# Last down products and second norm of a decoder layer: four equal column chunks, centred weights, row sums made in DRAM

## Chip, cores and metric

The kernel runs on one core of a Trainium2 chip. The metric is device time in microseconds, the median over the runs shown; the profile is of one more execution.

## The reference

One layer of a hybrid decoder, for a prompt of 1,024 tokens and 8 sample tokens that share the weights. Three branches (a gated recurrence, windowed attention, attention into 256 memory tokens) are merged, and then two post-norm steps follow. The change concerns the last of them:

```
h = layer_norm(ALPHA * x + merged @ w_out, ln1_g, ln1_b)
gt, up = jnp.split(h @ w_gate_up, 2, axis=-1)
h = layer_norm(ALPHA * h + (jax.nn.silu(gt) * up) @ w_down, ln2_g, ln2_b)
```

`layer_norm` takes mean and variance over the 1,024 features of each token. The inner width of the gated product is 2,816. All data are 32-bit floats.

## The kernel before, in words

Activations are held transposed: features on the 128 partitions (8 blocks m = 0 to 7 of the model width, 22 blocks of the inner width), tokens along the columns, T = 1,032 of them (1,024 and 8). A layer norm over features is thus a sum over partitions and blocks; it is done by a matrix product with a 128x128 matrix `ones` filled with 1/1024, which leaves the column's mean on every partition.

A product in full precision is done as three fast products: each operand is split into a high part (ScalarE casts, L79) and the rest (VectorE subtracts, L80), and `mm3` (L120 to L122) multiplies high by high, high by low and low by high.

`gate_up_down` (L1236) runs the gate and up products and most of the down product in *units* of a Strassen kind. A unit has seven steps i = 0 to 6 in two column halves, each of 12 products of 128x258 (L245 to L247), so 168 products. The units of the down product are (part, j), part 0 and 1, j = 0 to 3; each covers 8 of the 22 inner blocks and makes output rows 2j and 2j+1 in two tiles, za and zb. Steps put scaled partial results aside (p1s, p5s, u2s, ScalarE, L271) or add them into za and zb (VectorE, L273, L275 and L278; the last half of zb ScalarE, L1461). The PSUM bank that step 0 opened is used again by steps 2, 4 and 6; step 6 may overwrite it only when zb has been made from it by L275. In the profile `uf_6` and the like are the split weights of a step, d with some letters and digits is a split operand, `ubf`, `ucf`, `udf` are PSUM banks. `scr_h`, in DRAM, holds the residual; when za and zb are complete, GpSimd issues a DMA that accumulates each into its row of `scr_h` (`FinishDown.done`, L1465). Operands of the next part are loaded from `scr_f` (rows of the inner activation) and `scr_t` (sums of rows).

The last six inner blocks, 16 to 21, are done as plain products, in `last_products` (L1336). During the last ten steps of the units their inputs are prepared by hand-set steps (L1285 to L1291): six rows of `scr_f` are loaded and split (`last_rows`, L1310; tiles g5, g6, g7, named by the *home*, that is the buffers of finished operands that they take over), weight blocks are loaded by SP and split (`last_weights`, L1319; wl0 to wl7 raw, one per output block, in a ring of six raw buffers), and rows of `scr_h` are loaded as `acc` (`last_acc`, L1331). Then, for each of three column chunks (384, 390, 258) and each output block m, 18 products go to a PSUM bank `dl`, and VectorE adds it to acc (L1366). VectorE sums the rows of acc as it goes. The norm of a chunk (`layer_norm`, L951) runs beside the products of the next chunk: mean by `ones`, subtraction, squares, variance, root, reciprocal, scaling (L973), shift on ScalarE (L1354) and store (L1355).

The last chunk has `last_layer_norm` (L986), since no products follow to hide its norm. It takes an approximate mean away early, by `shift` products (L1013, L1014, L1023) from the first two rows; accumulates sums and sums of squares of what is left (VectorE L1004, GpSimd L1006); gets mean and mean square by `le` products (L1030 to L1033), the variance as a difference (L1037), then root (L1038), subtraction of the mean (L1040), reciprocal (L1041), scaling (L1044), shift and store.

What orders the work around the change: the hand-set steps above, `issue_after`, which puts norm pieces behind a named product on each engine, the ring of six raw weight buffers, ten buffers of 1,032 columns for za, zb and acc, and PSUM banks (`mm` 3, `s` 2, `t` 2, `o` 1). Each engine works its own instruction queue in order; SP and GpSimd issue DMAs in theirs.

Of the kernel before, what the change touches and what calls it, by code (L numbers as in the profile page):

```python
# [18 lines left out]
P = 128  # L19
# [7 lines left out]
WIDE = 400  # L27
# [8 lines left out]
LATE = 4  # L36
# [25 lines left out]
class Builder:  # L62
# [87 lines left out]
    def setup(self):  # L150
# [9 lines left out]
        self.shift = self.cst.tile([P, P], F32R, name="shift")  # L160
        nc.vector.memset(self.shift.bitcast(F32), -1.0 / (256 * SHARE))
# [789 lines left out]
    def layer_norm(self, c, r, s1, gcol, emit, name, late=False):  # L951


        nc, ph = self.nc, self.ph
        n = r[0].shape[1]
        yield
        mu = self.col_mean(s1, n, f"{name}mu{c}")
        s2 = ph.tile([P, WIDE], F32, tag="s2", name=f"{name}s2{c}", bufs=1)[:, :n]
        for m in range(KT):
            nc.vector.tensor_sub(r[m], r[m], mu)  # L960
            sq = s2 if m == 0 else ph.tile([P, WIDE], F32, tag="sq", name=f"{name}sq{c}_{m}", bufs=2)[:, :n]
            nc.scalar.activation(sq, r[m], AF.Square)
            if m:
                nc.vector.tensor_add(s2, s2, sq)
        yield
        var = self.col_mean(s2, n, f"{name}va{c}")
        rs = ph.tile([P, WIDE], F32, tag="rs", name=f"{name}rs{c}", bufs=1)[:, :n]
        nc.scalar.activation(rs, var, AF.Sqrt, bias=self.vec[:, V_EPS:V_EPS + 1])
        if late:
            yield  # L970
        nc.vector.reciprocal(rs, rs)
        for m in range(KT):
            nc.vector.scalar_tensor_tensor(r[m], r[m], self.vec[:, gcol + m:gcol + m + 1], rs, op0=ALU.mult,  # L973
                                           op1=ALU.mult)
            emit(m, r[m])

# [8 lines left out]

    def last_layer_norm(self, n, r, product, gcol, emit):  # L986


        nc, ph = self.nc, self.ph
        ones = self.ones.bitcast(F32)  # L990
        tile_ = lambda tag, name, bufs, dt=F32: ph.tile([P, WIDE], dt, tag=tag, name=name, bufs=bufs)[:, :n]
        s1, s2 = tile_("s1", "ls1", 1), tile_("s2", "ls2", 1)
        hi, lo = (t.rearrange("p k n -> p (k n)")[:, :n] for t in self.slot_pairs(4, "c0")[0])
        e1, e2 = self.bank("t", "le1")[:, :n], self.bank("t", "le2")[:, :n]

        def account(m):
            sq = s2 if m == 0 else tile_("sq", f"lsq{m}", 2)
            nc.scalar.activation(sq, r[m], AF.Square)
            if m == 7:
                return sq  # L1000
            if m == 1:
                nc.vector.tensor_add(s1, r[0], r[1])
            elif m:
                nc.vector.tensor_add(s1, s1, r[m])  # L1004
            if m:
                nc.gpsimd.tensor_add(s2, s2, sq)  # L1006

        for m in range(KT):
            ps = product(m, last=m < LATE)
            if m in NORM_AT:  # L1010
                self.norm_step()
            if m >= LATE:
                nc.tensor.matmul(ps, self.shift, hi, start=False, stop=False)  # L1013
                nc.tensor.matmul(ps, self.shift, lo, start=False, stop=True)  # L1014
            nc.vector.scalar_tensor_tensor(r[m], ps, SHARE, r[m], op0=ALU.mult, op1=ALU.add)
            if m == 1:
                s = tile_("xres", "lc0", 2)
                nc.vector.tensor_add(s, r[0], r[1])
                self.split(hi, lo, s)
            elif m == LATE - 1:  # L1020
                with self.tc.issue_after(self.last_mm):
# [591 lines left out]
```

## Time and profile before

| | us |
|---|---|
| median of 3 runs | 1939.35 (1938.84 to 1944.86) |
| profiled execution | 1941.62 |
| its span | 1939.8 |
| first of the last products | 1848.11 |
| last of the last products ends | 1919.43 |
| last store's affine ends | 1936.55 |

The span is what the profile covers, the profiled execution's own time is 1.8 us longer. Rows of a timeline give the start, the busy time, the engine, the line of the kernel, and output from inputs; in square brackets stands how long the engine was idle before and what ended that. Durations of TensorE's products overlap, so starts are to be compared rather than durations; VectorE's and ScalarE's overlap a little too.

### The profile page before, as it was taken

The page shows a single profiled execution, that of the slowest core. Times are in us where ns is not written, and L with a number is a line of the kernel's source. Part 1 is how long each engine was busy: PE and PEld are TensorE (multiplying, and loading weights), DVE is VectorE, ACT ScalarE, POOL GpSimd, SP SyncE. Part 2 cuts the span into 40 slices and gives each one's busy share as a digit, 9 for nine tenths or more (in the row PEclk, how much of TensorE's full clock was granted, in tenths as well). Part 3 has the DMA queues.
Part 4 walks back from the last instruction along what each step waited for, and adds up shares of the span by engine and source line. Part 5 has one row for each costly group of instructions (what it writes and reads, how often), then busy time and mean ns, then how long its engine had stood idle before and what let it go on. Part 6 is the DMA issues. An engine that isn't in the chain of part 4 may idle for free.

```text
span 1939.8 us, 37994 instructions
## 1 busy us (share of the span) xinstructions
PE 1902.9 (98%) x14716; PEld 1872.2 (97%) x14716; DVE 1388.3 (72%) x2738; ACT 1001.3 (52%) x2115; POOL 117.1 (6%) x168
## 2 busy tenths in 40 slices
PE   9999999999999999999999999999999999999996
PEld 9999999999999998988899999999999999999996
DVE  7878987887866655378887557785667667858467
ACT  6555565555655544388775224543433434636424
POOL 1000001110000000022210000000000000001001
PEclk9999999999999999999999999999999999999998
DMA  8545555445523376667534352123245245768542
GB/s 318 175 146 168 169 177 180 137 145 204 183 78 127 126 238 212 201 170 209 152 100 148 110 192 71 50 99 98 88 159 191 100 133 181 256 162 231 137 143 88
DMA packets 171637, 303.20 MB, mean 156 GB/s; under 512 B 19568, under 2 KB 86208, under 8 KB 171456
## 3 DMA queue, kind: packets, MB, share of 16 engines
q1 hardware_dynamic: 168384, 290.22, 45.6%
q0 software_dynamic: 3072, 10.55, 2.8%
q8 instruction: 115, 1.88, 0.4%
q14 instruction: 66, 0.54, 0.1%
HBM read 214.79 MB, written 90.09 MB: 157 GB/s over the span
## 4 chain that ended last, share of the span: by engine, by line
PE 86%; ACT 5%; DVE 4%; DMA 3%; issue 1%; ACTq 0%; SPq 0%; DVEq 0%; POOL 0%; POOLq 0%
PE ub L247 5%; PE ub L245 5%; PE ub L246 5%; PE ubfg L245 4%; PE ubfg L246 4%; PE ubfg L247 4%; PE ud L247 3%; PE ud L246 3%; PE ud L245 3%; PE udfg L245 2%; PE udfg L246 2%; PE udfg L247 2%; PE op L122 2%; PE op L120 2%; PE op L121 2%; PE brs L120 2%
## 5 line engine op out<-in xcount | busy, mean ns | idle before, releaser
L122 PE MATMUL op<-mh,wol 128*128 128x258 f32 x256 | 72.3, 282 | 1.3 <-DVE wol L80 1.3
L120 PE MATMUL op<-mh,woh 128*128 128x258 f32 x256 | 72.5, 283 | 0.0
L121 PE MATMUL op<-ml,woh 128*128 128x258 f32 x256 | 72.1, 282 | 0.0
L602 ACT ACTIVATE bp<-bp,bst 128x257 f32<-128x257 f32 (+1 forms) x128 | 62.8, 493 | 17.6 <-DVE bst L598 17.3
L245 PE MATMUL ub<-th,u_4h 128*128 128x258 f32 x240 | 67.8, 283 | 1.3 <-ACT u2s L271 1.3
L245 PE MATMUL ub<-th,u_0h 128*128 128x258 f32 x240 | 68.0, 283 | 0.6 <-ACT zb L1482 0.5
L247 PE MATMUL ub<-th,u_0l 128*128 128x258 f32 x240 | 68.2, 284 | 0.0
L247 PE MATMUL ub<-th,u_4l 128*128 128x258 f32 x240 | 68.2, 284 | 0.0
L247 PE MATMUL ub<-th,u_2l 128*128 128x258 f32 x240 | 68.2, 284 | 0.0
L247 PE MATMUL uc<-th,u_3l 128*128 128x258 f32 x240 | 68.2, 284 | 0.0
L247 PE MATMUL ud<-th,u_1l 128*128 128x258 f32 x240 | 68.2, 284 | 0.0
L247 PE MATMUL ud<-th,u_5l 128*128 128x258 f32 x240 | 68.1, 284 | 0.0
L247 PE MATMUL ub<-th,u_6l 128*128 128x258 f32 x240 | 68.1, 284 | 0.0
L245 PE MATMUL ub<-th,u_6h 128*128 128x258 f32 x240 | 68.0, 283 | 0.0
L245 PE MATMUL uc<-th,u_3h 128*128 128x258 f32 x240 | 67.9, 283 | 0.0
L245 PE MATMUL ub<-th,u_2h 128*128 128x258 f32 x240 | 67.8, 283 | 0.0
L245 PE MATMUL ud<-th,u_5h 128*128 128x258 f32 x240 | 67.8, 282 | 0.0
L245 PE MATMUL ud<-th,u_1h 128*128 128x258 f32 x240 | 67.7, 282 | 0.0
L246 PE MATMUL ub<-tl,u_6h 128*128 128x258 f32 x240 | 67.7, 282 | 0.0
L246 PE MATMUL ud<-tl,u_5h 128*128 128x258 f32 x240 | 67.7, 282 | 0.0
L246 PE MATMUL ub<-tl,u_4h 128*128 128x258 f32 x240 | 67.7, 282 | 0.0
L246 PE MATMUL ud<-tl,u_1h 128*128 128x258 f32 x240 | 67.7, 282 | 0.0
(946 smaller groups left out, 8221.9 us busy)
## 6 DMA issues: line engine op xcount, KB each, us to landing
ur<-win SPq DMA_DIRECT2D x120, 256.0 KB, 3.0
urfg<-wgu SPq DMA_DIRECT2D x80, 256.0 KB, 2.6
scr_f<-G SPq DMA_DIRECT2D x22, 516.0 KB, 3.3
f<-scr_f SPq DMA_DIRECT2D x16, 516.0 KB, 6.1
fs<-scr_t SPq DMA_DIRECT2D x16, 516.0 KB, 8.0
dck<-cmk SPq DMA_DIRECT2D x32, 256.0 KB, 3.5
dcv<-cmvT SPq DMA_DIRECT2D x32, 256.0 KB, 3.4
st<-scr_q SPq DMA_DIRECT2D x32, 256.0 KB, 5.4
```

Source lines behind the costliest of these rows:

```text
L120: nc.tensor.matmul(ps, sh, mh, start=opens and i == 0, stop=False)
L121: nc.tensor.matmul(ps, sh, ml, start=False, stop=False)
L122: self.last_mm = nc.tensor.matmul(ps, sl, mh, start=False, stop=closes and i == last).ins
L245: mm(sh[:, w], xh, start=opens and k == 0, stop=False)
L246: mm(sh[:, w], xl, start=False, stop=False)
L247: self.last_mm = mm(sl[:, w], xh, start=False, stop=k == 3).ins
L602: nc.scalar.activation(x, x, AF.Exp, bias=st[:, g:g + 1], scale=-1.0, accum_out=st[:, 4 + g:5 + g])
```

## The change

The last products go in four chunks of 258 columns. Three other things come with that.

The weights of the last six blocks are *centred*: for each inner row, the mean over the 1,024 outputs is taken away (`weight_means`: eight loads, eight reductions on VectorE, at steps 2 and 5 of gate units). `last_weights` then makes high and low parts with that mean as a bias, in pieces of 128 columns. So the last products have mean zero over the features.

The mean thus depends on the residual and the first two down parts only. Their row sums are made in DRAM: `row_sums` copies eight rows of `scr_h` into a new row `scr_r`, the first plainly and the rest by accumulating DMAs (at steps 0 and 3 of gate units), and `FinishDown.done` accumulates each za and zb into `scr_r` as well, except those of the last unit, which VectorE adds from the tiles. `centre` then takes the mean off the residual, ahead of the products or beside them.

The norm of a chunk (`down_norm`) is left with squares, variance, scaling, shift and store, done on tiles of four blocks (128x4x258). The last chunk's norm needs only the variance after its last product.

Core of the diff:

```diff
-CH = ((0, 384), (384, 390), (774, 258))
+            if i in (2, 5):
+                next(means, None)
+            if i in (0, 3):
+                next(rows, None)
...
-                step = {0: lambda: self.last_rows(5, 0), 3: lambda: self.last_rows(6, 2),
-                        4: lambda: self.last_rows(7, 4), 5: lambda: self.last_weights(0, 0),
-                        6: lambda: self.last_acc(0), 7: lambda: self.last_weights(1, 2),
-                        8: lambda: self.last_acc(1)}.get(n - len(todo) + 10)
+                step = {0: lambda: self.last_weights(5), 3: lambda: self.last_rows(6, 0),
+                        4: lambda: self.last_rows(7, 2), 5: lambda: self.last_rows(0, 4),
+                        6: lambda: self.last_weights(1), 7: lambda: self.last_weights(2),
+                        8: lambda: (self.residual(0, 0), self.residual(1, 0), self.last_weights(3))}.get(
+                            n - len(todo) + 10)
...
+    def row_sums(self):
+        nc = self.nc
+        for m in range(KT):
+            t = self.zt(f"rs{m}")
+            nc.sync.dma_start(t, self.scr["h"][:, m, :])
+            yield
+            nc.gpsimd.dma_start(self.scr["r"], t, **({"accum_op": ALU.add} if m else {}))
+            yield
...
-            for a, b in ((0, 512), (512, nf * P)):
-                raw = self.half_raw(self.io["wdn"][m][:, f0 * P + a:f0 * P + b], b - a, f"wl{m}r{a}")
-                self.split(hi[:, a:b], lo[:, a:b], raw[:, :b - a])
+            for a, b in ((0, 4), (4, nf)):
+                n = (b - a) * P
+                raw = self.half_raw(self.io["wdn"][m][:, (f0 + a) * P:(f0 + b) * P], n, f"wl{m}r{a}")
+                for k in range(a, b):
+                    w, r, c = slice(k * P, (k + 1) * P), raw[:, (k - a) * P:(k - a + 1) * P], self.wbar[:, k:k + 1]
+                    nc.scalar.activation(hi[:, w], r, AF.Identity, bias=c, scale=1.0)
+                    nc.vector.scalar_tensor_tensor(lo[:, w], r, c, hi[:, w].bitcast(F32), op0=ALU.add, op1=ALU.subtract)
...
+        s = self.ph.tile([P, T], F32, tag="rsum", name="rsum", bufs=1)
+        nc.sync.dma_start(s, self.scr["r"])
+        for z in self.tail:
+            nc.vector.tensor_add(s, s, z)
+        self.split(hi, lo, s)
+        self.mean = hi, lo
...
+    def centre(self, q):
+        nc = self.nc
+        mu = self.bank("o", f"n2mu{q}")[:, :QN]
+        for n, t in enumerate(self.mean):
+            nc.tensor.matmul(mu, self.ones, t[:, q * QN:(q + 1) * QN], start=n == 0, stop=n == 1)
+        for kh in range(2):
+            nc.vector.tensor_sub(self.A[q, kh], self.A[q, kh], self.spread(mu))
...
+                if q == 3:
+                    sq = s2 if m == 0 else ph.tile([P, QN], F32, tag="sq", name=f"lsq{m}", bufs=2)
+                    nc.scalar.activation(sq, r, AF.Square)
+                    if 0 < m < 7:
+                        nc.vector.tensor_add(s2, s2, sq)
+        ones = self.ones.bitcast(F32)
+        e = self.bank("t", "le")[:, :QN]
+        nc.tensor.matmul(e, ones, s2, start=True, stop=False)
+        nc.tensor.matmul(e, ones, sq, start=False, stop=True)
+        rs = row("lrs")
+        nc.scalar.activation(rs, e, AF.Sqrt, bias=self.vec[:, V_EPS:V_EPS + 1])
+        nc.vector.reciprocal(rs, rs)
+        for kh in range(2):
+            nc.vector.tensor_mul(self.A[3, kh], self.A[3, kh], self.spread(rs))
...
     def done(self, za, zb):
         for m, z in zip(self.rows, (za, zb)):
             self.b.nc.gpsimd.dma_start(self.b.scr["h"][:, m, :], z, accum_op=ALU.add)
+        if self.last:
+            self.b.tail = za, zb
+            return
+        for z in (za, zb):
+            self.b.nc.gpsimd.dma_start(self.b.scr["r"], z, accum_op=ALU.add)
```

How this stands in the queues is shown at two places. The first is VectorE in the last unit, from its first row split to zb; g5 to g7 and g0 are rows of `scr_f`, wl pieces are weights, `uf_6l` is the operand of step 6. Before:

```order
2446 L80 TENSOR_TENSOR g6l_23652<-g6l_23652,g6h_23651 128x1032
2447 L80 TENSOR_TENSOR wl0l_23742<-wl0r_23745,wl0h_23741 128x512
2448 L80 TENSOR_TENSOR uf_6l<-urf_11_23405,uf_6h 128x512
2449 L80 TENSOR_TENSOR g7l_23698<-g7l_23698,g7h_23697 128x1032
2450 L80 TENSOR_TENSOR wl0l_23742<-wl0r_23749,wl0h_23741 128x256
2451 L80 TENSOR_TENSOR g6l_23654<-g6l_23654,g6h_23653 128x1032
2452 L80 TENSOR_TENSOR wl0l_23744<-wl1r_23753,wl0h_23743 128x512
2453 L80 TENSOR_TENSOR g7l_23700<-g7l_23700,g7h_23699 128x1032
2454 L80 TENSOR_TENSOR wl0l_23744<-wl1r_23757,wl0h_23743 128x256
2455 L273 SCALAR_TENSOR_TENSOR zaf_23765<-ucf_0_23766,p1sf_0_23634 128x258
2456 L273 SCALAR_TENSOR_TENSOR zaf_23765<-ucf_1_23780,p1sf_1_23649 128x258
2457 L275 SCALAR_TENSOR_TENSOR zbf_23796<-ubf_0_23621,p5sf_0_23680 128x258
```

Now, from behind the first three row splits and `uf_6l`, which stand ahead of these rows (two splits of g6, one of g7; L269 and L271 are L273 and L275 of before):

```order
2463 L269 SCALAR_TENSOR_TENSOR zaf_23846<-ucf_0_23847,p1sf_0_23725 128x258
2464 L269 SCALAR_TENSOR_TENSOR zaf_23846<-ucf_1_23861,p1sf_1_23740 128x258
2465 L78 TENSOR_TENSOR g7l_23791<-g7l_23791,g7h_23790 128x1032
2466 L1264 SCALAR_TENSOR_TENSOR wl1l_23876<-wl2r_23879,wbar,wl1h_23875 128x128
2467 L78 TENSOR_TENSOR g0l_23833<-g0l_23833,g0h_23832 128x1032
2468 L1264 SCALAR_TENSOR_TENSOR wl1l_23876<-wl2r_23879,wbar,wl1h_23875 128x128 x2
2469 L78 TENSOR_TENSOR g0l_23835<-g0l_23835,g0h_23834 128x1032
2470 L1264 SCALAR_TENSOR_TENSOR wl1l_23876<-wl2r_23879,wbar,wl1h_23875 128x128
2471 L1264 SCALAR_TENSOR_TENSOR wl1l_23876<-wl2r_23889,wbar,wl1h_23875 128x128 x2
2472 L1264 SCALAR_TENSOR_TENSOR wl1l_23878<-wl3r_23895,wbar,wl1h_23877 128x128 x4
2473 L1264 SCALAR_TENSOR_TENSOR wl1l_23878<-wl3r_23905,wbar,wl1h_23877 128x128 x2
2474 L271 SCALAR_TENSOR_TENSOR zbf_23911<-ubf_0_23712,p5sf_0_23771 128x258
```

Two more splits of whole rows (g0) and twelve weight pieces now stand ahead of zb, in place of four weight pieces; the first two weights are split one unit earlier.

The second place is TensorE at step 6 of the last unit, which opens with `uf_6h`. Before, the products of step 5 (`uf_5`) stand directly ahead of it:

```order
13988 L247 MATMUL udf_1_23682<-d15h_22799,uf_5l 128x258
13989 L245 MATMUL udf_1_23682<-d15h_22799,uf_5h 128x258
13990 L246 MATMUL udf_1_23682<-d15l_22800,uf_5h 128x258
13991 L247 MATMUL udf_1_23682<-d15h_22799,uf_5l 128x258
13992 L245 MATMUL ubf_0_23621<-dth_0_22837,uf_6h 128x258
13993 L246 MATMUL ubf_0_23621<-dtl_0_22838,uf_6h 128x258
```

Now, the last of the seventeen products that stand in between:

```order
14004 L118 MATMUL dl_0_24096<-g0h_23832,wl5h_23604 128x258
14005 L119 MATMUL dl_0_24096<-g0l_23833,wl5h_23604 128x258
14006 L120 MATMUL dl_0_24096<-g0h_23832,wl5l_23605 128x258
14007 L118 MATMUL dl_0_24096<-g0h_23834,wl5h_23604 128x258
14008 L119 MATMUL dl_0_24096<-g0l_23835,wl5h_23604 128x258
14009 L241 MATMUL ubf_0_23712<-dth_0_22894,uf_6h 128x258
14010 L242 MATMUL ubf_0_23712<-dtl_0_22895,uf_6h 128x258
```

Seventeen of the eighteen products of the first output block of the first chunk have moved ahead of step 6; the eighteenth follows it.

More of the change, by code (lines that the diff above doesn't have):

```diff
@@ L949, in col_mean @@
         return ps
[L951 to L975, printed above, removed]
     def norm_step(self):
@@ L1417, in build @@
                 with ExitStack() as tx:
[L1418 removed]
+                    self.g, self.wl, self.A = [], [], {}
                     with pool("lnp") as self.ph:
@@ L1456, in __init__ @@
     def __init__(self, b, part, j):
-        self.b, self.rows = b, (2 * j, 2 * j + 1)
+        self.b, self.rows, self.last = b, (2 * j, 2 * j + 1), (part, j) == (FAST - 1, 3)
     def late(self, dst, ps):
```

211 lines of the change are left out of this document (102 added, 109 removed).

## The prediction

> **What bounds the kernel now.** I read the page first, the chain of waits next, then the timelines of the last unit and of the tail, and last a table of windows. The page's share of busy time and its chain name one engine:
>
> ```profile
> PE 1902.9 (98%) x14716; PEld 1872.2 (97%) x14716; DVE 1388.3 (72%) x2738; ACT 1001.3 (52%) x2115; POOL 117.1 (6%) x168
> PE 86%; ACT 5%; DVE 4%; DMA 3%; issue 1%; ACTq 0%; SPq 0%; DVEq 0%; POOL 0%; POOLq 0%
> ```
>
> So a microsecond counts where TensorE stands still. Ahead of the last products it hardly does; behind them it does to the end. The windows (columns: window and its length, busy PE, PEld, DVE, ACT and POOL, clock, DMA share, GB/s) cover the turn to the second down part (1740–1780), the last unit and the last products:
>
> ```profile
> core 0: us, PE busy (x) PEld busy (x) DVE busy (x) ACT busy (x) POOL busy (x), PEclk, DMA share, GB/s
> 1740.00:1760.00 20.00, 20.00 (x169) 20.00 (x169) 18.07 (x25) 14.10 (x23) 1.71 (x2) 1.00 0.97 300
> 1760.00:1780.00 20.00, 19.97 (x167) 19.77 (x166) 17.92 (x26) 14.12 (x23) 1.76 (x2) 1.00 0.94 293
> 1808.00:1828.00 20.00, 20.00 (x169) 20.00 (x168) 9.11 (x16) 7.04 (x15) 1.74 (x2) 1.00 0.44 91
> 1828.00:1832.00 4.00, 4.00 (x36) 4.00 (x35) 0.69 (x1) 1.69 (x4) 0.86 (x1) 1.00 1.02 256
> 1836.00:1840.00 4.00, 3.35 (x28) 3.15 (x27) 3.26 (x4) 4.00 (x9) 0.00 (x0) 1.00 0.75 301
> 1840.00:1844.00 4.00, 4.00 (x35) 4.00 (x35) 4.00 (x7) 3.31 (x6) 0.00 (x0) 1.00 0.53 132
> 1848.00:1856.00 8.00, 8.00 (x49) 8.00 (x48) 3.85 (x8) 1.72 (x4) 1.78 (x2) 1.00 1.03 319
> 1856.00:1864.00 8.00, 8.00 (x47) 8.00 (x46) 1.53 (x4) 1.86 (x4) 0.00 (x0) 1.00 1.04 322
> 1900.00:1920.00 20.00, 19.42 (x156) 18.77 (x154) 18.40 (x38) 8.48 (x18) 2.84 (x4) 1.00 0.01 1
> ```
>
> The reader should see two tight resources next to a full TensorE: the DMA engines (share about 1 in both stretches that load operands, 0.44 elsewhere) and VectorE (4.00 of 4 in 1840–1844, 18.40 of 20 before the end).
>
> **Part one, the tail (a gain).** From the last product to the end of the span at 1939.8:
>
> ```profile
> 1919.14 0.29 PE L1014 MATMUL dl<-c0l,shift 128*128 128x258 f32 x1
> 1919.67 0.41 DVE L1015 SCALAR_TENSOR_TENSOR acc<-dl,acc 128x258 f32<-128x258 f32 x1
> 1922.56 1.23 PE L1030 MATMUL le<-ls,ones 128*128 128x258 f32 x2 [3.14 <-DVE ls L1004]
> 1925.30 0.90 PE L1033 MATMUL le<-lsq,ones 128*128 128x258 f32 x2
> 1926.77 0.51 ACT L1038 ACTIVATE lrs<-lrs,vec 128x258 f32<-128x258 f32 x1
> 1928.69 1.75 DVE L1041 RECIPROCAL lrs<-lrs 128x258 f32<-128x258 f32 x1
> 1935.47 1.08 ACT L1354 ACTIVATE acc<-acc,vec 128x258 f32<-128x258 f32 x2
> 1936.09 1.09 SPq L1355 DMA_DIRECT2D o_y<-acc  x2
> ```
>
> It is 1939.8 − 1919.43 = 20.4 us. TensorE waits 3.14 us because VectorE, behind its row sums and the norm of the chunk before, is late; then come four row-sum products of two passes (0.90 each), the variance by subtraction, eight subtractions of the mean, and the 1.75 us reciprocal.
>
> Afterwards the mean is already out of the residual when the last product ends. What is left after that product: 0.65 for the PSUM result, 0.4 for its square, 1.9 for the last sums and two row-sum products, 0.6 for the root, 1.75 for the reciprocal, 2.4 for two scalings of 1032 columns (1.15 apart, row below), 1.6 for the affines that follow the second scaling in turn on two engines, and 3.25 for the last store (1936.55, the end of L1354, to 1939.8). The sum is 12.5 us. **Gain 7.9 us**; if the last sums overlap less well or better, 7 to 9. No row shows a 1032-column scaling by a broadcast row; it lies between one such pass (1.15) and four of 258 columns (4 x 0.33), which agree.
>
> **Part two, the products.** The first product of each chunk:
>
> ```profile
> 1848.11 0.34 PE L120 MATMUL dl<-g5h,wl0h 128*128 128x384 f32 x1
> 1873.26 0.34 PE L120 MATMUL dl<-g5h,wl0h 128*128 128x390 f32 x1
> 1899.57 0.28 PE L120 MATMUL dl<-g5h,wl0h 128*128 128x258 f32 x1
> ```
>
> Chunk one: 25.15 us for 144 products of 384 columns, 0.1747 each, or 2,198 columns per us. The window 1808–1828 has 169 products of 258 columns in 20.00 us, 0.1183 each, or 2,181. So narrow products cost no more per column. Now the stage lasts 1919.43 − 1848.11 = 71.3 us. Afterwards: 576 x 0.1183 = 68.1, and 14 row-sum products of 258 columns, 1.7. That leaves 1.5 us for waits before it is even. I put 1.2 there (the last chunk lost about that now: 19.86 us for 154 of its own and 2 for the norm of the chunk before, 18.5), and take **−0.3**, between −1.3 and +2. Centring, folding and scaling stand in VectorE's order behind the PSUM results, and the window 1856–1864 has it busy 1.53 of 8, so they have room.
>
> **Part three, the last unit (a cost).** Its step i=6 waits for zb on VectorE, and ahead of that zb stand the splits of rows and weights. Rows of VectorE, ScalarE and TensorE there:
>
> ```profile
> 1840.74 1.24 DVE L80 TENSOR_TENSOR g6l<-g6l,g6h 128x1032 fp32r<-128x1032 f32 x1
> 1841.89 0.68 DVE L80 TENSOR_TENSOR wl0l<-wl1r,wl0h 128x512 fp32r<-128x512 f32 x1
> 1842.49 1.23 DVE L80 TENSOR_TENSOR g7l<-g7l,g7h 128x1032 fp32r<-128x1032 f32 x1
> 1843.64 0.42 DVE L80 TENSOR_TENSOR wl0l<-wl1r,wl0h 128x256 fp32r<-128x256 f32 x1
> 1843.97 0.42 DVE L273 SCALAR_TENSOR_TENSOR zaf<-ucf,p1sf 128x258 f32<-128x258 f32 x1
> 1844.64 0.74 DVE L275 SCALAR_TENSOR_TENSOR zbf<-ubf,p5sf 128x258 f32<-128x258 f32 x2
> ...
> 1835.57 1.05 ACT L79 CAST g6h<-g6l 128x1032 fp32r<-128x1032 f32 x1 [3.75 <-DMA g6l<-scr_f]
> 1840.59 0.64 ACT L79 CAST wl0h<-wl1r 128x512 fp32r<-128x512 f32 x1
> 1841.11 1.08 ACT L79 CAST g7h<-g7l 128x1032 fp32r<-128x1032 f32 x1
> ...
> 1839.23 0.39 PE L245 MATMUL ubf<-dth,uf_4h 128*128 128x258 f32 x1 [0.65 <-ACT u2sf L271]
> 1845.12 0.38 PE L245 MATMUL ubf<-dth,uf_6h 128*128 128x258 f32 x1
> ```
>
> Starts on VectorE lie 1.15 apart at 1032 columns, 0.60 at 512, 0.33 at 256; the line through the last two gives 0.2 at 128 columns (an estimate), and 0.33 is the most. Before, zb comes after four rows (4.6), four weight pieces (1.86), one operand (0.6) and two za (0.67). After, six rows (6.9) and 12 pieces of 128 columns (2.4, at most 4.0) stand there: +2.85, at most +4.45. VectorE is full from 1836.7 to 1845.06, so zb's first half is done at 1847.9, at most 1849.5, if the rows come in time.
>
> [...]
>
> On SP's queue five weight loads (1.15 MB, 3.8 us at 301 GB/s) now stand ahead of these rows. They run before 1828, where the share is 0.44, so I cost them at nothing; without that room they would cost the rows 3.8 us. Two more rows have to be loaded, and accumulating DMAs to the new row compete with them:
>
> ```profile
> q0 software_dynamic: 1152, 4.23, 15.1%
> scr_h<-zbf POOLq DMA_DIRECT2D x4, 516.0 KB, 7.8
> ```
>
> The first line is POOL's queue over 1780–1941, eight accumulating DMAs: 15.1% of 161 us / 8 = 3.0 us of all 16 engines each. One or two of them fall between 1828 and 1844 (3.0 to 6.1), the two rows are 1.03 MB at 301 GB/s (3.4); 1836–1844 has 0.25 x 4 + 0.47 x 4 = 2.9 us free. The loads there end near 1839 now, so then at 1842.5 to 1845.6. Behind the last row come its cast (1.05), its subtraction (1.15), nine pieces (1.8) and zb (0.4): 1846.9 to 1850.0.
>
> Against that, TensorE's order has 17 of the first tile's 18 products ahead of i=6 (2.0 us that fill the wait). So I take zb at 1849, i=6 starts there with 2.0 us of the next stage done, that is as at 1847.0 instead of 1845.12: **+2**, from −0.65 (the wait at i=4 goes and no new one comes) to +5 (both DMAs in the way, pieces at 0.33).
>
> **Part four, small items.** The weight sums and the copies of rows to the new DRAM row run in gate units, with a whole unit's time each and 2 DMAs per step: 0, covered by TensorE's work; if that cover fails, the 8 accumulations cost 3.0 us of DMA each. In units (0,0) to (1,2) 14 more of them follow the za and zb of each unit; and units (1,1) and (1,2) get the splits of two weights between casts that TensorE needs, 0 to 2 us; together **+0.5**. The mean needs the last load of SP's queue (the row, behind the last weights, which wait for VectorE behind zb) and three adds and a split; TensorE reaches the first mean product 3.0 + 8 x 2.1 = 20 us after zb, and the row must be there some 15 us after zb. I put **+0.7** (0 to 4) there.
>
> **Sum:** −7.9 − 0.3 + 2 + 0.5 + 0.7 = −5.0. The profiled execution took 1941.6 (span 1939.8), so 1936.6; the median of the runs shown is 1939.35, 2.3 lower, so 1934.4. About 0.3%, 5.8 us, is what a measurement here can tell from no change.
>
> **The rivals.** *First, the cover holds:* rows land early, the pieces cost 0.2, and the wait at i=4 goes. For it: 1808–1828 has a DMA share of 0.44, and the weights are now loaded before the rows. Then −7.9 − 0.65 − 0.3 + 0.5 = −8.35, 1931.0.
>
> *Second, the accumulating DMAs reach the path (slower).* In 1740–1780 four more of them take 12.1 us where 0.03 x 20 + 0.06 x 20 = 1.8 are free; 3.4 go with the two rows no longer loaded there, leaving 7. The operands have slack:
>
> ```profile
> 1763.31 1.06 ACT L79 CAST dth<-fs 128x1032 fp32r<-128x1032 f32 x1 [1.71 <-DMA fs<-scr_t]
> 1777.84 0.28 PE L245 MATMUL ubf<-dth,uf_4h 128*128 128x258 f32 x1
> ```
>
> This one is cast at 1763.3 and used at 1777.8, which is against the rival: delays under 12 us are hidden. In the last 40 us before 1864 there is no such slack: 6.1 for two accumulations, 3.4 for rows and 1.5 for the new row's load against 2.9 free is 8. If all 7 + 8 reach TensorE: −7.9 − 0.3 + 15 = +7, 1946. It decides from about 14 us of delay beyond the free share. [...]
>
> *Third, the mean comes late:* the row lands after 1866, the mean product waits at the head of TensorE's order, and all tiles behind it with it. SP's queue there is 1.9 MB behind zb (5.9 us alone, 12 shared with POOL's residuals and accumulations, 16 at worst). Price 4 to 6: −5 − 0.7 + 5 = −0.7, no change, 1938.7.
>
> **How the numbers follow.** Forecast 0.45 (1931 to 1938; a third of it beyond −5.8), first rival 0.28 (beyond it nearly always), third 0.13, second 0.14 (slower by over 0.3% in most of it, with worse sums of parts three and four). Faster 0.44, within 0.3% 0.43, slower 0.13. The range leaves out the best of the first rival and most of the second's upper end: 1929.5 to 1945.5.
>
> **What the new profile would show.** Right: last product to end of span about 12.5 us; the last stage 70 to 73 us; a wait of 1 to 4 us of TensorE for zb before i=6, with 17 products ahead of it. The first rival would show no wait there; the second, waits of casts for scr_f or scr_t and TensorE idle in 1760–1790; the third, the first mean product waiting for VectorE's split of the row sum. A tail over 15 us or a wait in a gate unit would make the prediction wrong in a step that I did not price.

## The result, and the profile after

The changed kernel takes 1959.23 us (median, 1956.89 to 1963.32), the kernel before, run beside it, 1942.11 (1938.84 to 1945.04). The ratio is 1.0095, with an interval from 1.0083 to 1.0108: slower by 17 us, where 5 us faster was forecast and 1945.5 was the end of the range. The profiled execution took 1963.32 us, its span is 1961.5, so 21.7 us over the span before. It is the slowest of the four, 4.1 us over their median.

The page's busy times, its chain and POOL's queue, in the changed kernel:

```profile
PE 1908.6 (97%) x14852; PEld 1877.8 (96%) x14852; DVE 1391.2 (71%) x2740; ACT 1007.9 (51%) x2140; POOL 131.7 (7%) x184
q0 software_dynamic: 6832, 24.29, 6.5%
PE 78%; DMA 9%; ACT 5%; DVE 5%; issue 2%; SPq 0%; POOL 0%; DVEq 0%; ACTq 0%; POOLq 0%
```

TensorE's part of the chain falls from 86% to 78%, and DMA's grows from 3% to 9%: transfers end more of the waits on that chain. The time is in TensorE's timeline. These are all its waits of 0.8 us and more behind the gate units (first column the start, in brackets the wait and what ended it), with the first and the last of the last products:

```profile
1776.77 0.58 PE L241 MATMUL ubf<-dth,uf_0h 128*128 128x258 f32 x1 [6.06 <-ACT zbf L1481]
1833.35 0.39 PE L241 MATMUL ubf<-dth,uf_4h 128*128 128x258 f32 x1 [2.66 <-ACT u2sf L267]
1857.07 0.58 PE L241 MATMUL ubf<-dth,uf_4h 128*128 128x258 f32 x1 [4.69 <-ACT u2sf L267]
1865.32 0.28 PE L118 MATMUL dl<-g6h,wl5h 128*128 128x258 f32 x1
1870.12 0.39 PE L241 MATMUL ubf<-dth,uf_6h 128*128 128x258 f32 x1 [2.31 <-DVE zbf L271]
1892.88 0.39 PE L1309 MATMUL n2mu<-rsumh,ones 128*128 128x258 f32 x1 [2.14 <-ACT rsumh L77]
1894.15 0.58 PE L1309 MATMUL n2mu<-rsuml,ones 128*128 128x258 f32 x1 [0.88 <-DVE rsuml L78]
1947.92 0.28 PE L120 MATMUL dl<-g0h,wl3l 128*128 128x258 f32 x1
1949.44 0.70 PE L1378 MATMUL le<-s,ones 128*128 128x258 f32 x2 [1.23 <-DVE s L1375]
```

The first is at the turn of the parts, in step 0 of part 1's first unit. The next two are at step 4 of its last two units, and 2.31 is at step 6 of the last.

What held zb at the turn stands in ScalarE's timeline:

```profile
1766.82 1.05 ACT L77 CAST dth<-fs 128x1032 fp32r<-128x1032 f32 x1 [5.63 <-DMA fs<-scr_t]
1770.31 1.05 ACT L77 CAST dth<-fs 128x1032 fp32r<-128x1032 f32 x1 [1.91 <-DMA fs<-scr_t]
1772.39 1.05 ACT L77 CAST d15h<-f1TrueTrue 128x1032 fp32r<-128x1032 f32 x1 [1.03 <-DMA f1TrueTrue<-scr_f]
1775.38 1.05 ACT L77 CAST d15h<-f1TrueTrue 128x1032 fp32r<-128x1032 f32 x1 [1.41 <-DMA f1TrueTrue<-scr_f]
1776.33 0.38 ACT L1481 ACTIVATE zbf<-ubf 128x258 f32<-128x258 f32 x1
```

The operands dth and d15h are not wanted before steps 4 and 5. But zb, for which TensorE waits now, stands behind their casts in the same queue. It had no slack in the kernel before either: there it starts right behind the last of these casts, and TensorE's next product, which follows at 0.12 us elsewhere, comes 0.31 after the one at 1767.37:

```profile
1767.25 0.38 ACT L1461 ACTIVATE zbf<-ubf 128x258 f32<-128x258 f32 x1
1767.68 0.39 PE L245 MATMUL ubf<-dth,uf_0h 128*128 128x258 f32 x1
```

In the changed kernel the other two places read alike (u2s behind a weight piece, u2s behind a row's cast):

```profile
1831.81 0.40 ACT L1263 ACTIVATE wl5h<-wl0r,wbar 128x128 fp32r<-128x128 f32 x1 [3.39 <-DMA wl0r<-wdn]
1832.92 0.38 ACT L267 ACTIVATE u2sf<-ubf 128x258 f32<-128x258 f32 x1
...
1854.89 1.05 ACT L77 CAST g6h<-g6l 128x1032 fp32r<-128x1032 f32 x1 [9.31 <-DMA g6l<-scr_f]
1856.64 0.38 ACT L267 ACTIVATE u2sf<-ubf 128x258 f32<-128x258 f32 x1
```

Why the loads are late shows in part in the windows that the prediction used (same columns), in the changed kernel:

```profile
1740.00:1760.00 20.00, 20.00 (x169) 20.00 (x169) 14.25 (x20) 13.50 (x23) 2.65 (x3) 1.00 1.05 321
1760.00:1780.00 20.00, 13.94 (x105) 13.75 (x104) 14.10 (x21) 9.83 (x15) 3.49 (x4) 0.84 0.95 268
1808.00:1828.00 20.00, 20.00 (x168) 20.00 (x167) 8.89 (x19) 6.65 (x16) 3.51 (x4) 1.00 0.75 144
```

The DMA engines are about as full in 1740–1780 as before (0.97 and 0.94), with more to move, and GB/s falls from 293 to 268 in 1760–1780. The stretch that had a share of 0.44 has 0.75.

At the turn something else comes first. SP, which issues these loads, waits there itself (its queue's row, then its wait: us in total, times, longest):

```profile
1762.77 9.25 SPq L1096 DMA_DIRECT2D f1TrueTrue<-scr_f  x2
SPq L1096 <- DMA scr_r<-zbf: 8.4, 1, 8.4
```

The kernel takes za, zb and these rows from one ring of ten buffers, and the second row of d15h waits until the accumulation of a zb has left its buffer. SP issues the row at 1771.64, 0.05 us after that accumulation has landed; it is there at 1775.35, and its cast and zb follow in the rows above. The kernel before has no such wait. The last unit is another case: there SP issues g6's first row at 1842.17 after a wait of 0.3 us for TensorE only, but 12.7 us pass until its cast, where it was 7.1 before.

The differences of the starts of the same steps in both traces give this ledger: +3.0 us up to the turn (2.1 of it ahead of the gate units, in code that both kernels share, so no effect of the change), +7.7 at the turn, +2.9 in the unit of 1833, +6.4 and +2.8 at steps 4 and 6 of the last unit (the second without the seventeen products that moved there), +5.9 in the rest of the last stage, −7.1 in the tail (13.3 us from 1948.2 to the end, before 20.4). The sum is 21.6 of 21.7.

### The profile page after: what moved, and what is told of

Same layout as the page of the kernel before. It is cut to its first block, busy times and chain, and to the rows that moved or that the text cites. A ratio compares the mean times of both kernels' runs of the same rounds, so it can differ in the third digit from the quotient of the medians.

```text
span 1961.5 us, 38304 instructions
## 1 busy us (share of the span) xinstructions
PE 1908.6 (97%) x14852; PEld 1877.8 (96%) x14852; DVE 1391.2 (71%) x2740; ACT 1007.9 (51%) x2140; POOL 131.7 (7%) x184
## 4 chain that ended last, share of the span: by engine, by line
PE 78%; DMA 9%; ACT 5%; DVE 5%; issue 2%; SPq 0%; POOL 0%; DVEq 0%; ACTq 0%; POOLq 0%
PE ub L241 5%; PE ub L243 5%; PE ub L242 5%; PE ubfg L242 4%; PE ubfg L241 4%; PE ubfg L243 4%; PE ud L243 2%; PE ud L241 2%; PE ud L242 2%; PE udfg L241 2%; PE udfg L242 2%; PE udfg L243 2%; PE brs L118 2%; PE brs L119 2%; PE brs L120 2%
## 5 line engine op out<-in xcount | busy, mean ns | idle before, releaser
L241 PE MATMUL ub<-th,u_6h 128*128 128x258 f32 x240 | 68.1, 284 | 0.0
L241 PE MATMUL uc<-th,u_3h 128*128 128x258 f32 x240 | 68.1, 284 | 0.0
L242 PE MATMUL uc<-tl,u_3h 128*128 128x258 f32 x240 | 67.5, 281 | 0.0
L242 PE MATMUL ub<-tl,u_0h 128*128 128x258 f32 x240 | 67.4, 281 | 0.0
L242 PE MATMUL ub<-tl,u_2h 128*128 128x258 f32 x240 | 67.4, 281 | 0.0
```

Source lines behind the costliest of these rows:

```text
L241: mm(sh[:, w], xh, start=opens and k == 0, stop=False)
L242: mm(sh[:, w], xl, start=False, stop=False)
```

## The experiments

Each was timed beside the kernel before; ratios are to that one. The first question was whether the accumulations into the new row make the waits, or the new order and its small weight pieces.

**Without the fourteen accumulations of za and zb.** The mean lacks the down parts' share; all else stays.

```diff
-        for z in (za, zb):
-            self.b.nc.gpsimd.dma_start(self.b.scr["r"], z, accum_op=ALU.add)
```

> The changed kernel without the 14 accumulating DMAs that add za and zb of the down units to the new row (their part of the mean is left out of the result); the copies of the residual's rows, the centred weights, the order and the tail stay. Theory A (these accumulations delay operand loads, by DMA time and by the buffers they hold): the waits at the turn of the parts (7.2 us), in unit (1,2) (2.9) and at i=4 of the last unit (6.4) go or shrink to before's 0.7, so 12 to 17 us below the changed kernel's 1959, 1942 to 1947. Theory B (the order: splits for the last products stand between casts that TensorE needs): only the wait at the turn goes, 1951 to 1953.

Measured: 1941.13 us, ratio 0.9997 (0.9987 to 1.0007). Of TensorE's waits in the changed kernel only this one is left, besides the 1.23 us in the tail:

```profile
1852.95 0.38 PE L241 MATMUL ubf<-dth,uf_6h 128*128 128x258 f32 x1 [2.31 <-DVE zbf L271]
```

The waits of 6.06, 2.66, 4.69 and 3.02 us (2.14 and 0.88, for the mean) are gone with fourteen DMAs, and so is SP's wait for the buffer. A new one of 1.99 us stands in a gate unit at 1448; ahead of it VectorE waits 3.37 us for a load of the weight sums and 2.09 for rows of the inner activation.

**Weights split as before, in 512 and 256 columns, uncentred** (so the mean lacks the last blocks' part).

```diff
-                for k in range(a, b):
...
+                self.split(hi[:, a * P:b * P], lo[:, a * P:b * P], raw[:, :n])
```

> The changed kernel with the last weights split as before, in pieces of 512 and 256 columns and not centred (the mean of the products is thus left in); all DMAs stay. Theory A: 0 to 1 us less, 1958 to 1959, with the same waits at i=4. Theory B: the pieces on ScalarE and VectorE cost part of the waits in units (1,2) and (1,3), so 3 to 6 us less, 1953 to 1956.

Measured: 1958.85, ratio 1.0086 (1.0070 to 1.0103), with the waits at the same places (6.89, 3.17, 2.46, 3.19, and 1.21 for the mean). The pieces are not the cause.

**The kernel before, with nothing but the fourteen accumulations added** (into a row that nobody reads).

```diff
+        for n, z in enumerate((za, zb)):
+            self.b.nc.gpsimd.dma_start(self.b.scr["r"], z, **({"accum_op": ALU.add} if n or not self.first else {}))
```

> The kernel before, with nothing but the 14 accumulations of za and zb into a row of DRAM added, which nobody reads. Theory A: waits appear at the turn of the parts (6 to 7 us) and at i=4 of the last unit (2 to 5), 1949 to 1955. Theory B: the turn alone, or nothing, 1942 to 1949.

Measured: 1954.72, ratio 1.0072 (1.0053 to 1.0092). Its TensorE waits at the same two steps, with no other part of the change there:

```profile
1773.63 0.58 PE L245 MATMUL ubf<-dth,uf_0h 128*128 128x258 f32 x1 [6.17 <-ACT zbf L1461]
1850.68 0.58 PE L245 MATMUL ubf<-dth,uf_4h 128*128 128x258 f32 x1 [4.88 <-ACT u2sf L271]
```

SP's wait for the buffer is there as well (8.1 us). So the fourteen DMAs cost 14 us by themselves (10 to 18 by the interval). The next three ask by which way.

**Two rows in place of one.** Each zb's accumulation into the row waits on POOL until za's has landed, and holds its buffer for that long. The waits of the changed kernel say it (us in total, times, longest):

```profile
POOL scr_r L1490 <- DMA scr_r<-zaf: 48.4, 7, 8.4
```

Here za and zb go to rows of their own, with the same bytes.

```diff
-            self.b.nc.gpsimd.dma_start(self.b.scr["r"], z, accum_op=ALU.add)
+            self.b.nc.gpsimd.dma_start(self.b.scr["r"][:, n, :], z, accum_op=ALU.add)
```

> The changed kernel with two new rows in DRAM, za accumulated into the one and zb into the other, so that zb's accumulation need not wait for za's; the bytes are the same, and at the end one more row is loaded and added. If the wait at the turn comes from buffers that are held until zb's accumulation ends (it starts 8 us after za's), it goes: 5 to 7 us less, 1952 to 1954. If it comes from DMA time alone: the same as the changed kernel within 1.5 us, or up to 3 us more for the added row.

Measured: 1959.42, ratio 1.0089 (1.0074 to 1.0104). The wait at the turn halves to 3.10 us, as SP's falls to 5.0:

```profile
SPq L1096 <- DMA scr_r<-zbf: 5.0, 1, 5.0
```

The other waits stay (2.30, 5.10, 2.23) or grow (3.92 for the mean, with one more row to load), and the median doesn't move. With the same bytes, the hold of a buffer thus decides about half of the turn's wait; this run shortens that hold and does not end it. The loss in the last units is not of this kind.

**Accumulations of part 0 only** (the mean lacks part 1).

```diff
+        if self.part == 0:
```

> The changed kernel with only the eight accumulations of the first down part's za and zb; the six of the second part are left out (and missing from the mean). If each wait is made by the accumulations that run beside it: the wait at the turn (6 to 7 us) stays, those at i=4 in units (1,2) and (1,3) go, 1947 to 1950. If the delay of the turn carries on through the queues: waits in (1,2) and (1,3) stay too, 1953 to 1958.

Measured: 1946.05, ratio 1.0025 (1.0014 to 1.0036). The wait at the turn stays, and SP's with it (8.5 us); those of part 1's units go, except the 2.31 us at step 6:

```profile
1773.91 0.58 PE L241 MATMUL ubf<-dth,uf_0h 128*128 128x258 f32 x1 [6.81 <-ACT zbf L1481]
```

Each wait is made by the accumulations beside it.

**Plain writes in place of accumulations**, from the same queue and of the same size, to a row that nobody reads (the mean lacks both parts).

```diff
-            self.b.nc.gpsimd.dma_start(self.b.scr["r"], z, accum_op=ALU.add)
+            self.b.nc.gpsimd.dma_start(self.b.scr["w"], z)
```

> The changed kernel with the 14 accumulations of za and zb replaced by plain writes of the same tiles into another row, also from GpSimd's queue, in the same places and one after the other (the mean lacks these parts). Same number of DMAs, same buffers held, but a plain write moves the bytes once, about 1.5 us of all DMA engines instead of 3.0. Theory DMA time: at most half of the 18 us stays, 1943 to 1951. Theory count or held buffers: nearly all stays, 1955 to 1960.

Measured: 1947.04, ratio 1.0023 (1.0010 to 1.0036). No wait at the turn is over 0.3 us; six of 0.3 to 1.2 us and the 2.31 remain. POOL's queue on the pages of this run and of the one without the fourteen, whose spans are 1945.8 and 1939.4:

```profile
q0 software_dynamic: 6832, 24.29, 5.5%
```

```profile
q0 software_dynamic: 4816, 16.89, 4.5%
```

5.5% of 1945.8 less 4.5% of 1939.4 is 19.7 us, so a plain write takes 1.4 us of all 16 engines. In the changed kernel 6.5% of 1961.5 less the same 87.3 is 40.2, so an accumulation takes 2.9, twice as much. Half the engine time leaves about a third of the cost (5.9 of 18 us). At the turn this run doesn't part engine time from held buffers, because a plain write lands sooner as well: SP waits 4.1 us for the buffer in place of 8.4. In the last unit, where SP waits for no such buffer, engine time is what is left: from the issue of g6's first row to its cast it is 12.7 us in the changed kernel, 8.3 here and 5.3 without the fourteen.

**The queue or the operand?** TensorE waited for zb behind casts. To test whether the order on ScalarE is the cause, the splits of operands 4 to 6 were written behind the first steps of part 1, with loads and accumulations unchanged.

```diff
+            if u == (1, 0) and i < 3:
+                self.operand_split(*self.held[i + 4])
```

> The changed kernel with one thing moved: at the turn of the parts the splits of the operands 4, 5 and 6 of part 1 stand behind the first, second and third step of its first unit on ScalarE and VectorE, not in the steps before, so that zb of part 0's last unit no longer stands behind them; loads and accumulations stay. Theory (the wait of 6.06 us at the turn is zb in the queue behind casts whose rows come late, not the operands being late for their own products): the wait falls under 1 us and nothing of its size comes later in that unit; the other waits stay; the time is 1950 to 1954, 6 to 9 us under the changed kernel. Rival (the operands are late in themselves, since the DMA engines are full): a wait of 3 to 6 us comes at steps 4 to 6 of the first unit in its place and the time stays at 1957 to 1961.

Measured: 1958.06, ratio 1.0094 (1.0077 to 1.0112), with 5.26 us at the turn. This says nothing on the order: in ScalarE's timeline the casts stand ahead of zb again. Written once more, with the splits tied behind those steps:

```diff
+            if part == 1 and i > 3:
+                self.behind(ins, self.last_small)
```

> The run before this one of the same idea only wrote the splits later, and the scheduler put them back ahead of zb, so it tested nothing. Here the splits of operands 4, 5 and 6 of part 1 are tied behind the first three steps of its first unit on ScalarE, so zb stands ahead of them; loads, accumulations and bytes are those of the changed kernel. Theory (queue): TensorE's wait at the turn falls from 6.06 us to under 1 us, no wait of its size takes its place in that unit, the others stay; 1950 to 1954 us. Rival (the operands are late in themselves): a wait of 3 us or more at steps 4 to 6 of that unit, 1957 to 1961 us.

Measured: 1960.20, ratio 1.0099 (1.0085 to 1.0112). Now zb is made at 1764 and 1766, without a wait, and the wait at step 0 is gone. But one of 8.30 us takes its place at step 4. TensorE, VectorE and SP's queue in this run:

```profile
1785.84 0.58 PE L242 MATMUL ubf<-dtl,uf_4h 128*128 128x258 f32 x1 [8.30 <-DVE dtl L78]
```

```profile
1783.22 0.69 DVE L225 TENSOR_TENSOR usf<-urf,urf 128x512 f32<-128x512 f32 x1 [13.83 <-DMA urf<-wdn]
1784.56 2.37 DVE L78 TENSOR_TENSOR dtl<-fs,dth 128x1032 fp32r<-128x1032 f32 x2
```

```profile
1759.40 9.36 SPq L1096 DMA_DIRECT2D f1TrueTrue<-scr_f  x2
...
1770.80 26.32 SPq L93 DMA_DIRECT2D urf<-wdn  x6
```

The operand's rows were there (cast at 1769.4 and 1770.6). Its subtraction stands behind a weight sum of the next unit, whose weights it waits 13.83 us for. SP issues those from 1770.80 on, behind two rows of `scr_f` that take it 9.36 us; 8.4 of these are the same wait for zb's buffer. The theory failed. The rival was right on the place of the wait and on the time, but not on the reason, since the rows of the operand itself were there. So ScalarE's order is not the cause alone: SP's loads are as late as before, and another queue holds what TensorE needs behind one of them.

**The same at every place.** The whole changed kernel with splits tied behind u2s in the last two units too, zb ahead of g0 and the weight pieces, weight sums earlier, and the first mean two output blocks later.

```diff
+            self.behind(self.split(hi, lo, lo.bitcast(F32)), self.last_small)
+            if zb:
+                self.behind(self.last_lo, zb)
```

> The changed kernel, whole, with all its accumulations, and only the order of queues mended: operands 4 to 6 tied behind the first steps of the new part as in the other run; the first split weights and the last rows' splits tied behind u2s of their units; zb ahead of g0 and the weight pieces on VectorE; weight sums made earlier; the mean of chunk 0 wanted two output blocks later, that of chunk 2 two later. Theory (the accumulations cost time only through queues that stand behind their late loads): the waits of 6.06, 2.66, 4.69, 2.31 and 3.02 us fall to under 1 us each or go; 1937 to 1943 us. Rival (the DMA engines are full in the last 100 us, so some load becomes the bound wherever the casts stand): waits of 2 to 5 us at the last rows or weights in their place, 1946 to 1955 us.

Measured: 1957.98, ratio 1.0083 (1.0070 to 1.0097). The waits at u2s and the mean are gone, and 8.87, 1.45, 5.12, 1.68 and 2.13 us stand elsewhere. The rival is right in kind, though the time is above its range: these ties move the waits and don't remove them. SP's wait for the buffer (7.9 us) is still there; a run with the accumulations and without that wait was not made.

**What is the tail worth without them?** The run without the fourteen accumulations, with zb ahead of the weight pieces in the last unit and the weight sums a step earlier (the mean lacks the down parts):

```diff
+            if i in (0, 2, 5):
...
+                        7: lambda: (self.last_weights(1), self.last_weights(2)),
```

> This is the run without the accumulations into the row sums (the part of the mean that comes from the down products is left out) with two further moves: the weight sums are made at earlier steps, and in the last two units the copy zb stands ahead of the weight pieces on VectorE. Theory (accumulations cost the time; the tail term of 7 us is real and two small waits, 2.3 us at i=6 of the last unit and 2.0 us at the gate matrix of 1448, give part of it back): both waits go and the time is 1936 to 1938, some 4 us under the kernel before. Rival (the weight pieces, now behind zb and behind the residual loads on SP, come late instead, at the first down products of the last unit): the waits only change place and the time is 1940 to 1942, the same as before.

Measured: 1936.04, ratio 0.9976 (0.9968 to 0.9985), faster than before by 4.7 us. Two waits are left, and these rows open and close its last stage (span 1933.0):

```profile
1845.70 0.28 PE L118 MATMUL dl<-g6h,wl5h 128*128 128x258 f32 x1
1858.51 0.36 PE L118 MATMUL dl<-g6h,wl2h 128*128 128x258 f32 x1 [1.82 <-DVE r L1370]
1920.12 0.28 PE L120 MATMUL dl<-g0h,wl3l 128*128 128x258 f32 x1
1921.63 0.70 PE L1378 MATMUL le<-s,ones 128*128 128x258 f32 x2 [1.24 <-DVE s L1375]
```

The tail takes 1933.0 − 1920.4 = 12.6 us.

**Can a whole result have it?** Six attempts, one of them with a fault in its result, and none beats the kernel before. Two make the row sums from the final residual on VectorE, with no row in DRAM; the second makes the last weights a step later:

```diff
+        self.nc.vector.tensor_add(t, self.A[q, 0], self.A[q, 1])
+        self.rs[q] = self.fold(t)
```

> The changed kernel without the row in DRAM at all: no copies of the residual's rows, no accumulations. VectorE folds the eight residual blocks of a chunk beside the products (about 2.1 us a chunk, 8.4 in all) and the mean comes from that; the result is complete. If the accumulations were the whole loss: at or a little below the run without them (1941), 1938 to 1942. If folding holds up the products: above 1943.

Measured: 1944.78, ratio 1.0011 (1.0003 to 1.0020). VectorE is late for the last sums (4.02 us).

> As the run with folding, and two more moves: the weights' preparation of the last unit is one step later, so that on VectorE zb stands ahead of the twelve weight pieces, and the weight sums are done by unit 8 of the gate units, three steps a unit, before the sums of the first down part's rows begin. If the wait of 2.3 us at i=6 and that of 2.0 us in a gate unit go, 3 to 5 us below the run with folding, 1934 to 1938, better than before; if new waits take their place, within 1 us of it.

Measured: 1943.28, ratio 1.0005 (0.9994 to 1.0016), the best whole one. The wait for zb goes, 2.65 us for the last weights come, and 4.03 at the last sums stay. With the residual loads behind the weights (a fold buffer is used again too early there, so the mean of a chunk is taken from another chunk):

> As the run with folding and later weights, with two of its own new waits taken up: on SP's queue the last weight loads stand ahead of all residual tiles but the first (the products waited 2.65 us for a weight there), and the residuals of chunks three and four are folded and centred four to six products earlier (the row-sum product waited 4.0 us behind VectorE, 1.2 in the changed kernel). If both go: 4 to 5 us below that run's 1943, 1937 to 1940, which is 3 to 5 below the kernel before. If VectorE is simply too full in the last chunk, the second stays and the time is 1940 to 1942.

Measured: 1946.28, ratio 1.0035 (1.0023 to 1.0047); now the residual is late (2.87 us) and the last sums 5.64. Next, row sums in an SBUF tile, added by GpSimd, which costs one of the ten buffers:

```diff
-            self.b.nc.gpsimd.dma_start(self.b.scr["r"], z, accum_op=ALU.add)
+            self.b.nc.gpsimd.tensor_add(self.b.rsum, self.b.rsum, z)
```

> The changed kernel with its row of sums held in SBUF and summed by GpSimd (24 additions of 128x1032, an estimate of 3.5 us each from its 0.89 us for 258 columns) in place of the copies and accumulations in DRAM; one buffer fewer (9 for 10) for the row tiles, later weights and their loads as in the other run. The result is complete and VectorE has no folding to do. If only DMA time was at fault: no waits at the turn or at i=4, tail of 13 us, 1935 to 1939. [...]

Measured: 1959.29, ratio 1.0086 (1.0074 to 1.0098), with waits of 4.20 us in a gate unit and 7.31 for the residual. It mixes the sums with one buffer less and another order of loads, so it says nothing on either alone. Last, GpSimd folds for chunks 1 to 3, first with the residual loaded late, then in the changed kernel's order:

> A whole result without accumulations into row sums: the residual is folded into the parts' sum ahead of the row sums, on VectorE for chunk 0 and on GpSimd for chunks 1 to 3; residuals of chunks 2 and 3 are loaded on SP after earlier products; zb ahead of the weight pieces; weight sums earlier. Theory (the four-chunk tail is worth about 7 us and only the accumulations spoil it): no wait over 1 us at the turn, the first down products or the row sums, and 1936 to 1940, under the kernel before by 2 to 6 us. Rival (the tail's gain needs VectorE or the loads, which are full in the last 60 us): waits of 2 to 4 us at the weight pieces or the last row sums remain and the time is 1942 to 1946.

Measured: 1946.51, ratio 1.0024 (1.0012 to 1.0036); the first mean waits 6.28 us for rows that land at 1874.5.

> A whole result without accumulations into the row sums, made from the run with zb first: the loads stay in the changed kernel's order, the parts' residual is folded to row sums by VectorE for chunk 0 and by GpSimd for chunks 1 to 3, and the mean of chunk 0 is wanted three output blocks later. Theory (the tail's gain is there for a whole result if the mean needs neither further DMAs nor VectorE time where it is full): waits near those of the run with zb first, 1936 to 1939. Rival (the mean needs the last residual rows, which land some 8 us after the last accumulations, and the folds hold those rows while VectorE wants them): a wait of 3 us or more at the means or at r, 1941 to 1946.

Measured: 1945.59, ratio 1.0024 (1.0016 to 1.0033); waits of 2.74 and 6.55 us for r; ahead of the second VectorE waits 13.0 us for GpSimd's folds of the same rows. Here the rival was right too. The whole mean cost at least what the tail gave wherever it was paid; that it must is not shown.

## Why the prediction was wrong, step by step

**The step that failed** stands in the second rival: "This one is cast at 1763.3 and used at 1777.8, which is against the rival: delays under 12 us are hidden." The slack was the operand's own. What counts is the slack of all that stands behind its cast in the queue, and zb had none: TensorE lost 7.7 us there. The tied run shows that the slack was no longer there in the next queue either. A second part of the delay no step names: an accumulation keeps its buffer until it has landed, and SP's queue stood behind that for 8.4 us.

The rival, to which I gave 0.14, was right that these DMAs reach the path, and its sign came: casts that wait for `scr_t` and `scr_f`, and TensorE idle in 1760–1790. Its price, 7 + 8 = 15 us, was near the 14 that they cost when added to the kernel before alone, in part by luck: the 8 counts rows and a load that this run doesn't have, and the 7 at the turn is engine time alone, where the same engine time in two rows gave a wait of 3.10 us instead of 6.06. Yet the sum took +0.5 for them. The price per accumulation (3.0 us by the row, 2.9 measured) was right.

The last unit, the rival's other place, shows such a delay too: SP's load of g6's row takes 12.7 us to its cast beside POOL's accumulations and 5.3 without the fourteen.

**A cost that no step had.** After three of the waits TensorE also runs slower for a while. Windows behind the waits of 6.06 and 4.69 us, and behind one of 2.31, with the granted clock third from the end:

```profile
1770.00:1780.00 10.00, 3.94 (x22) 3.75 (x21) 6.68 (x9) 7.22 (x11) 2.62 (x3) 0.69 0.84 257
```

```profile
1857.00:1861.00 4.00, 3.93 (x18) 3.93 (x19) 2.04 (x3) 2.36 (x5) 0.00 (x0) 0.50 1.02 340
1870.00:1873.00 3.00, 2.88 (x23) 2.89 (x24) 3.00 (x13) 2.57 (x9) 0.00 (x0) 1.00 0.90 278
```

At clock 0.50 products start 0.215 us apart instead of 0.12, for 3.7 us behind the turn's wait: 17 x 0.095 = 1.6 us more. That is the step from 6.06 to 7.7. It comes again for 5.3 us behind 4.69 and for 5.5 behind the two waits for the mean, about 2.3 and 2.4 us more. Each of these three stretches ends with 3.41 us in which TensorE doesn't stand still. The length of the idle time ahead does not tell by itself where one starts: in the run with zb first 1.82 us were followed by one (products from 1859.3 to 1862.7 stand 0.215 apart), while 2.31 and 2.66 us here were not.

The traces show what half clock goes with. In each of them the stretches at half clock start whole multiples of 3.41 us apart (here at 1773.71, 1855.63 and 1893.18, 24 and 11 of them). From 1300 us to the last product, in all 18 traces, 37 of these windows at full clock have 1.82 us of idle TensorE or more, and half clock follows every one of them; it follows none of those with 1.80 or less. The 2.31 us at step 6 fall into two windows here, 1.5 and 0.8; in the run without the fourteen a wait of the same length lies in one, and the clock halves behind it:

```profile
1854.00:1857.00 3.00, 3.00 (x16) 3.00 (x15) 3.00 (x13) 2.67 (x10) 0.00 (x0) 0.50 1.04 343
```

**The tail** (−7.9, 12.5 us) was right: 12.6 in the undisturbed run, 13.3 in the changed kernel.

**The products** (−0.3) were too low. Part of that is the price of one, 0.1183 us: the window's 169 counts products that start before it or end behind it. A whole unit there, from 1806.70 to 1826.90, has 168 in 20.20 us, 0.1202 each, so 576 take 69.3 us and not 68.1. The rest is waits. In the run with zb first the last stage takes 74.7 us (1845.70 to 1920.40), in the kernel before 71.3. 1.8 of the 3.4 is the wait for r, 1.5 the slower clock behind it. In the changed kernel the mean's waits take their place.

**The last unit** (+2) had the right wait, 2.31 us at step 6 for zb behind rows and pieces, in the changed kernel and, at 2.2 to 2.3, in the runs that keep this order and the pieces. It is as forecast and no part of the miss. Without the fourteen, moving zb forward and mending the weight sums' wait brought 1941.13 down to 1936.04. The wait at step 4 was expected to go ("the wait at i=4 goes and no new one comes" was the low end); it grew from 0.65 to 4.69, since ScalarE waits 9.31 us for g6's row, and u2s stands behind its cast.

**The weight pieces** (0.2 us by the line) start 0.26 apart: in the run with zb first six take 1.66 us. **The small items** (+0.5) are the accumulations above, **the mean** (+0.7, 0 to 4) 3.0 us of wait and 2.4 of slow clock. The third rival's mechanism thus came as well, and it goes when the accumulations go.

## What to carry to other kernels

A transfer that nobody waits for was not free where the DMA engines were full (fourteen cost 14 us, added to the kernel before, whose DMA share in 1740–1780 is 0.94 to 0.97): take its engine time off the free share first, and add what is left to the sum. Then ask which load takes its buffer next, and what stands behind that load in its queue. The slack of a late operand is that of the tightest instruction behind its cast in the same queue (zb at the turn, 6.06 us of wait), in every queue that touches it (dtl in the tied run, 8.30). Reordering can merely move such a wait: two tied orders here changed the time by about 1 us, while fourteen DMAs less saved 18 us. The tied orders left the buffers and SP's order as they were.

## What the runs showed of the hardware that I had not expected

- An accumulating DMA of 516 KB to DRAM takes 2.9 us of all 16 engines, a plain write of the same tile 1.4.
- The hold of a buffer by an accumulation kept SP's whole queue waiting: 8.4 us until the accumulation of a zb had landed, 5.0 with two rows, 4.1 with plain writes.
- TensorE's clock halved by windows of 3.41 us: behind each with 1.82 us of idle time or more, behind none with 1.80 or less. So idle times of 2.31 us halved it in one run and not in another.
- GpSimd adds a 128x1032 tile of 32-bit floats in 2.4 to 3.3 us (2.75 in the median of 21 rows of the run with sums in SBUF), where VectorE's subtractions of that size start 1.15 apart.
